# Nine tiles for one ring of raw and compression weights, and an order by due times for DVE, ACT and the load queue

## The chip, the cores and the metric

The kernel runs on one core of a Trainium2 chip. The core has a matrix engine (TensorE, PE in the profile), a vector engine (VectorE, DVE), a scalar engine (ScalarE, ACT), a general one (GpSimd, POOL, hardly used here) and a sync engine (SyncE, SP) from which this kernel issues its loads. Each engine takes its instructions from a queue of its own, in the order in which they were written there, and waits on semaphores for the others. The metric is the device time of one execution in microseconds (us); lower is better.

## What is computed

Two layers, each a token mixer and a squared-ReLU MLP, with RMS norms before and after each, on 256 tokens of width 1024 in float32. The reference, cut to what matters here:

```python
h = rms_norm(x, g_pre_mix)
y = h @ w_in                       # 2848 columns: q, six k/v groups, gates, FoX q, k, v, forget logits
# NSA heads: 8 query heads on 2 k/v heads, three branches added by sigmoid gates
kc = gelu((blocks(k_c) + pos_k) @ w1_k + b1_k) @ w2_k + b2_k     # compressed keys, 15 blocks of 32
vc = gelu((blocks(v_c) + pos_v) @ w1_v + b1_v) @ w2_v + b2_v
o_cmp = masked_softmax(q @ kc.T) @ vc
o_sel = masked_softmax(rope(q) @ rope(k_s).T) @ v_s    # blocks chosen by the compressed scores
o_win = masked_softmax(rope(q) @ rope(k_w).T) @ v_w
# FoX heads: 8, causal attention with a cumulated log forget gate
o_fox = masked_softmax(fq @ fk.T + cum[:, None] - cum[None, :]) @ fv
x = x + rms_norm(concat(o, o_fox) @ w_out, g_post_mix)
h = rms_norm(x, g_pre_mlp)
x = x + rms_norm(square(relu(h @ w_up)) @ w_down, g_post_mlp)
```

With 256 tokens there are four blocks for the selection and 16 may be chosen, so every block is chosen. The window of 512 covers all tokens as well.

## The kernel before

**Precision.** A float32 product is made as three products of a faster type: each operand is split into a high part and a rest, and hi·hi, hi·lo and lo·hi are added up in PSUM (`mm3`). Activations are split once. For weights ACT writes `whi`, a rounded copy of the raw tile, and DVE writes `wlo`, raw minus `whi`, for every weight unit.

**Weights.** All weights come as a list of units in the order in which they are used, most of them 128 partitions by 1024 columns (512 KB). The class `Weights` (from line 414) gives them out: `get(i)` records the load of unit i, unless it was recorded already, and its split. The loads go to SP's queue. A raw unit lands in a tile of the ring with the tag "raw", which has four tiles (`RBUFS`); whi and wlo have seven tiles each (`WBUFS`). The weights of the compression (`w1k` and `w1v`, four units each in a layer) are used by PE as they are, without a split, in one stretch of 16 matmuls each. They have a ring of their own, tag "w1", of four tiles. Their loads are tied to a place in the program by `nc.after` (lines 433 to 443), with the leads `RIDE_LEAD` and `FAR_LEAD`; the units of w1k ride with the four units of chunk 2 of the input projection, those of w1v with chunk 3.

**Stages of a layer.** The columns of `w_in` are cut into six chunks, of which each has four units (the very first chunk eight). Chunks 3 and 4 give the FoX queries and keys transposed (`in_chunk_T`), the others come by token (`in_chunk`), and `evac` functions take them out of PSUM. The rotated queries (`q_rot`: a high part by ACT, a rest by DVE) are transposed by PE, and so are the compressed scores (`csT`, in a tile with the tag "pcT", after `compressed_scores`). Then a loop over 24 score steps (16 for NSA, 8 for FoX) interleaves scores, softmax, transposes and products with the values (`scores`, `scale`, `probs_T`, `pv`); the tiles of probabilities form a ring of three. In its gaps `fill` puts matmuls of the input projection that remain. After that come the output projection, the norms and gains (`pre_gain`, `sandwich`) and the MLP, eight groups of 512 columns.

**Order.** Nothing is put on an engine as the program is written. A `Recorder` (from line 169) writes down every operation with its engine, a `key` (by default its place in the program; loads and splits get the key of an earlier place, `LOAD_LEAD` and `SPLIT_LEAD` units ahead), a cost, the operations that it depends on and the buffers that it uses. Buffers of a ring are given out in order of first use in the program. `order()` (lines 245 to 343) then plays the four queues (tensor, vector, scalar, sync) through at build time, with estimated costs: whenever an engine is free, it takes the operation with the lowest key among those that are ready and whose buffers are free; operations marked urgent come first. `emit` (line 345) writes each engine's instructions in that order. This is why nearly every instruction has line 352 in the profile, and why the profile is read by tile names. The choice stands in one line:

```python
if op.ready <= t and (best is None or (best.urgent, -best.key) < (op.urgent, -op.key)) and fits(op):
```

Of the kernel before, what the change touches and what calls it, by code (L numbers as in the profile page):

```python
# [18 lines left out]
F32 = mybir.dt.float32  # L19
# [5 lines left out]
P = 128  # L25
D = 1024
S = 256
# [5 lines left out]
NEG = -1e30  # L33
LASTK = 4
LANE = 0.9
WAIT = 0.7
WARM = 4
RETILE = 145
# [2 lines left out]
FIRSTS = [(k, k + 1) for k in range(8)]  # L41
NFIRST = 768
UPK = 7
TOK, WBUFS, RBUFS = 6, 7, 4
LOAD_LEAD, SPLIT_LEAD, RIDE_LEAD, FAR_LEAD = 12, 1, 6, 20
OPERANDS = ("whi", "wlo", "xT", "act0", "act1", "qT", "kx0", "kx1", "raw", "w1", "gain", "tok", "rl",
            "pr", "prT", "x0", "x1", "fV", "cum", "cs", "pcT", "vbig", "vS", "vW", "kstk", "kstv", "rT")
EPS = 1e-6

# [67 lines left out]
class Buf:  # L117


    def __init__(self, pool, shape, dtype, name, tag, bufs, psum):  # L120
        self.pool, self.shape, self.dtype, self.name, self.tag, self.bufs = pool, shape, dtype, name, tag, bufs
        self.psum, self.real = psum, None
        self.size = int(np.prod(shape[1:]))
        self.writes, self.reads, self.ops = [], [], 0
# [38 lines left out]

class Op:
    __slots__ = ("engine", "name", "args", "kw", "key", "urgent", "cost", "deps", "succs", "bufs",
                 "missing", "ready", "start", "end", "tile")


class Recorder:
# [21 lines left out]
    def add(self, engine, name, args, kw):  # L191
# [7 lines left out]
        if self.lane is not None and self.key is None:  # L199
            op.key = self.lane + LANE * (len(self.ops) - self.lane)  # L200
        op.urgent = self.hot
# [40 lines left out]
            d.succs.append(op)  # L242
        self.ops.append(op)

    def order(self):


        free = {tag: q[0].bufs for tag, q in self.fifo.items()}
# [25 lines left out]
        def fits(op):  # L274
            taken = {}
            for b in op.bufs:
                if b not in live:
                    n = taken.get(b.tag, 0)
                    if free[b.tag] <= n or self.fifo[b.tag][head[b.tag] + n] is not b:
                        return False  # L280
                    taken[b.tag] = n + 1
            return True
# [3 lines left out]
        count, out, live = 0, [], set()  # L286
        while events:
            t, _, released = heapq.heappop(events)
            if released is not None:
                free[released] += 1  # L290
            if events and events[0][0] == t:
                continue
            for e, ops in waiting.items():
                while busy[e] <= t:
                    best = None
                    for op in ops:
                        if op.ready <= t and (best is None or (best.urgent, -best.key) < (op.urgent, -op.key)) and fits(op):
                            best = op
                    if best is None:
                        break  # L300
                    if not best.urgent and e != "tensor" and not force:
                        q = hot[e]
                        while q and q[0].start is not None:
                            q.popleft()
                        memo = {}
                        if any(estimate(op, memo) < t + WAIT * best.cost for op in list(q)[:4] if op.start is None and fits(op)):
                            break
                    ops.remove(best)
                    for b in best.bufs:
                        if b not in live:  # L310
                            live.add(b)
                            free[b.tag] -= 1
                            head[b.tag] += 1
                    best.start = t
                    out.append(best)
                    if e == "sync":
                        busy[e] = t + 450
                        bus = max(bus, t + 1150) + best.cost
                        best.end = bus + 900
                    else:  # L320
                        busy[e] = best.end = t + best.cost
                        if e == "tensor" and best.tile != tiled:
                            tiled = best.tile
                            busy[e] = best.end = best.end + RETILE
                    count += 1
                    heapq.heappush(events, (busy[e], count, None))
                    for b in best.bufs:
                        left[b] -= 1
                        if not left[b]:
                            count += 1  # L330
                            heapq.heappush(events, (best.end + (260 if b.psum else 150), count, b.tag))
                    for s in best.succs:
                        s.ready = max(s.ready, t, best.end + s.deps[best])
                        s.missing -= 1
                        if not s.missing:
                            waiting[s.engine].append(s)
                            count += 1
                            heapq.heappush(events, (s.ready, count, None))
            force = not events and len(out) < len(self.ops)
            if force:  # L340
                heapq.heappush(events, (t + 100, 0, None))
# [72 lines left out]
class Weights:  # L414


    def __init__(self, nc, tile, units, one, far):
        self.nc, self.tile, self.units = nc, tile, units
        self.raw, self.marks = {}, []

        self.one, self.far = one, far

    def load(self, i):
        kind, shape, src = self.units[i]
        self.raw[i] = (self.tile([P] + shape, F32, name="w1", tag="w1", bufs=4) if kind == "raw" else
                       self.tile([P] + shape, F32, name="wraw", tag="raw", bufs=RBUFS))
        self.nc.sync.dma_start(self.raw[i], src)

    def get(self, i):
        nc, marks = self.nc, self.marks  # L430
        assert len(marks) == i
        marks.append(len(nc.ops))
        if i not in self.raw:
            nc.key = marks[max(i - LOAD_LEAD, 0)]
            far = i in self.far
            if self.units[i][0] == "raw":


                lead = FAR_LEAD if far else RIDE_LEAD
                nc.after = nc.ops[marks[i - lead] - 1] if i > self.one else self.last  # L440
                nc.key = marks[i - lead] if far else nc.key
            self.load(i)
            self.last, nc.after = nc.ops[-1], None
        kind, shape, src = self.units[i]
        raw = self.raw.pop(i)
        nc.key = None
        if kind == "raw":
            return raw
        nc.key = marks[max(i - SPLIT_LEAD, 0)]
        hi = self.tile([P] + shape, F32R, name="whi", tag="whi", bufs=WBUFS)  # L450
        lo = self.tile([P] + shape, F32R, name="wlo", tag="wlo", bufs=WBUFS)
        for j in range(shape[0]) if i < len(FIRSTS) else [slice(None)]:
            if i:
                nc.scalar.activation(hi[:, j], raw[:, j], AF.Copy)
            else:

                nc.vector.tensor_copy(hi[:, j], raw[:, j])
            nc.vector.tensor_sub(lo[:, j], raw[:, j], hi[:, j].bitcast(F32))
        nc.key = None
        return hi, lo  # L460
# [14 lines left out]
def trunk(nc, A, consts_in, out, sbp, pp):  # L475
    def tile(shape, dtype, name, tag=None, bufs=1):
        return nc.tile(sbp[(tag or name) not in OPERANDS], shape, dtype, name, tag, bufs)

# [3 lines left out]
    def small(shape, name, bufs=2):  # L482
        return tile(shape, F32, name=name, tag=name, bufs=bufs)


    units, index = [], {}
# [14 lines left out]
    for l in range(DEPTH):  # L501
        at = 0
        for c, (a, b) in enumerate(CHUNKS):
            w_in = A["w_in"][l][:, at:at + 8 * (b - a)].rearrange("p (k n) -> p k n", k=8)
            at += 8 * (b - a)
            for q, (k0, k1) in enumerate(parts_of(l, c)):
                add_unit((l, "in", c, q), [k1 - k0, b - a], w_in[:, k0:k1, :])
                if (c, q) in RIDES:
                    s, j = RIDES[c, q]
                    w1 = A["cmp_w1_" + s][l].rearrange("p (k n) -> p k n", k=16)  # L510
# [18 lines left out]
            for q in range(4):  # L529
                add_unit((l, "dn", fc, q), [1, D], wd[:, 4 * fc + q:4 * fc + q + 1, :])  # L530

    W = Weights(nc, tile, units, index[0, "out", 0], [index[1, "w1k", j] for j in range(4)])

    def weight(*key):
        return W.get(index[key])
# [13 lines left out]
    for k in range(8):  # L549
# [8 lines left out]
        a = 8 + k * NFIRST - o  # L558
# [172 lines left out]
    xT = new_xT()  # L731
# [14 lines left out]
    for l in range(DEPTH):  # L746
        first = l == 0
# [9 lines left out]
        T = {}  # L757
# [174 lines left out]
        def compressed_scores():  # L932
            ps = psum("s")
            with nc.stretch():
              for p in range(4):
                nc.tensor.matmul(ps[32 * p:32 * p + 32, :S], kbd[:, p // 2].rearrange("p j n -> p (j n)"),
                                 T["qT"][:, p, :], start=True, stop=True, tile_position=(0, 32 * p))
            T["csT"] = small([P, S], "pcT", 1)
            nc.scalar.activation(T["csT"], ps[:, :S], AF.Copy)

        def compressed_exp():
# [343 lines left out]
        for i in range(len(flat) + 4):  # L1285
# [14 lines left out]
            j = i - 3  # L1300
            if 0 <= j < len(flat) and flat[j][2] == 1 and flat[j][3] != 1:
                kind, pair, par, br = flat[j]
# [18 lines left out]
        xT = new_xT()  # L1321
# [106 lines left out]
        for fc in range(8):  # L1428
# [21 lines left out]
            if not last_l:  # L1450
                xT = new_xT()
# [63 lines left out]
```

## Time and profile before

| what | value |
|---|---|
| three runs, median (lowest to highest) | 628.62 us (628.45 to 632.04) |
| the profiled execution | 630.89 us |
| its span in the profile | 629.1 us |
| mean granted clock of TensorE | 0.999 |
| HBM read over the span | 114.00 MB |

The profile shows one execution. Its span leaves out 1.8 us of the time at both ends. A matmul of PE is pipelined with the next and its end is modelled, so the sum of shown durations is more than the distance from one start to the next; distances between starts are the better measure. In rows with tile names, `a<-b,c` is an operation that writes a from b and c; `x2` counts instructions put together in one row. In brackets stands the idle time of the engine just before the row and the operation or transfer that ended it.

### The profile page before, as it was taken

Reading aid. Unit: us, or ns where it says so; the run is one execution under the profiler, and the core shown is the slowest. Engines: PE = TensorE matmul, PEld = TensorE weight load, DVE = VectorE, ACT = ScalarE, POOL = GpSimd, SP = SyncE. Lnnn points to the kernel's source line nnn. Section 1 sums busy time; section 2 is a strip of 40 time slices with the busy share of each in tenths; the row PEclk is TensorE's granted clock in tenths of the full one; section 3 lists DMA queues with packets and bytes.
Section 4 is the critical chain, followed back from the end, with each engine's and each line's share of the span. In section 5 each row is a group of like instructions: output and inputs, shape, how many; then the busy total and the mean of one; then the engine's idle time right before and its main releaser. Section 6 shows DMA issues by size and latency. Waiting matters only on the chain.

```text
span 629.1 us, 9912 instructions
## 1 busy us (share of the span) xinstructions
PE 617.4 (98%) x3572; PEld 518.3 (82%) x3572; DVE 482.4 (77%) x1077; ACT 375.8 (60%) x736; POOL 0.2 (0%) x4
## 2 busy tenths in 40 slices
PE   9999999999999999999999999999999999999995
PEld 7877977788888888888888888777888888888884
DVE  6878999969986566566598999996998666566544
ACT  7855757664865455456468656764767565455432
POOL 0000000000000000000000000000000000000000
PEclk9999999999999999999999999999999999999999
DMA  8986344305777556658326943533268656566501
GB/s 319 379 310 218 100 145 148 130 34 203 236 250 250 195 178 203 193 178 290 122 75 222 329 163 106 158 108 101 68 218 282 220 188 205 187 182 202 190 1 67
DMA packets 33600, 115.69 MB, mean 184 GB/s; under 512 B 3984, under 2 KB 4112, under 8 KB 33552
## 3 DMA queue, kind: packets, MB, share of 16 engines
q1 hardware_dynamic: 33552, 115.07, 55.6%
q8 instruction: 28, 0.46, 0.3%
q14 instruction: 20, 0.16, 0.1%
HBM read 114.00 MB, written 1.05 MB: 183 GB/s over the span
## 4 chain that ended last, share of the span: by engine, by line
PE 81%; DVE 7%; DMA 6%; ACT 4%; issue 1%; DVEq 0%; SPq 0%; ACTq 0%
PE s L352 34%; PE acc L352 24%; PE x L352 18%; DMA wraw<-in_w_in_dram 5%; PE o L352 5%; DVE wlo L352 3%; ACT whi L352 2%; DMA first<-in_first_dram 1%; DVE pr L352 1%; DVE x L352 1%; DVE m L352 1%; ACT xT L352 1%; DVE mg L352 0%; ACT rl L352 0%; DVE rsqrt L352 0%
## 5 line engine op out<-in xcount | busy, mean ns | idle before, releaser
L352 DVE TENSOR_TENSOR wlo<-wraw,whi 128x1024 fp32r<-128x1024 f32 (+1 forms) x188 | 225.0, 1202 | 85.1 <-ACT whi L352 81.9
L352 ACT ACTIVATE whi<-wraw 128x1024 fp32r<-128x1024 f32 (+1 forms) x188 | 194.8, 1041 | 129.3 <-PE acc L352 59.8
L352 PE MATMUL s<-xT,whi 128*128 128x512 f32 x448 | 112.0, 392 | 0.0
L352 PEld LDWEIGHTS s<-xT,whi 128*128 128x128 f32 x448 | 81.5, 189 | 15.1
L352 PE MATMUL acc<-whi,aT 128*128 128x512 f32 x256 | 88.7, 390 | 0.0
L352 PE MATMUL x<-whi,aT 128*128 128x512 f32 x256 | 88.5, 390 | 0.0
L352 PEld LDWEIGHTS s<-xT,wlo 128*128 128x128 f32 x448 | 61.1, 191 | 4.4
L352 PE MATMUL s<-xT,wlo 128*128 128x256 f32 x448 | 62.5, 282 | 0.0
L352 PEld LDWEIGHTS acc<-whi,aT 128*128 128x128 f32 x256 | 48.0, 188 | 9.9
L352 PEld LDWEIGHTS x<-whi,aT 128*128 128x128 f32 x256 | 48.1, 188 | 9.6
L352 ACT ACTIVATE pr<-pr,st 128x128 f32<-128x128 f32 (+1 forms) x96 | 42.8, 448 | 18.1 <-DVE st L352 17.7
L352 PE MATMUL acc<-xT,whi 128*128 128x256 f32 x256 | 50.1, 288 | 0.2 <-DVE fqT L352 0.2
L352 PE MATMUL x<-wlo,aT 128*128 128x512 f32 x128 | 50.0, 391 | 0.0
L352 PE MATMUL acc<-wlo,aT 128*128 128x512 f32 x128 | 49.9, 390 | 0.0
L352 PEld LDWEIGHTS acc<-xT,whi 128*128 128x128 f32 x256 | 40.6, 190 | 2.9 <-issue 1.2
L352 PE MATMUL x<-whi,xT 128*128 128x512 f32 x112 | 37.0, 403 | 0.2 <-ACT xT L352 0.2
L352 PE MATMUL acc<-xT,wlo 128*128 128x256 f32 x128 | 36.3, 284 | 0.0
L352 PE MATMUL acc<-whi,xT 128*128 128x512 f32 (+1 forms) x128 | 35.7, 353 | 0.1
L352 ACT ACTIVATE rl<-x 128x512 f32<-128x512 f32 x24 | 14.7, 614 | 24.9 <-PE x L352 16.7
L352 PEld LDWEIGHTS acc<-wlo,aT 128*128 128x128 f32 x128 | 24.0, 188 | 4.9
L352 PEld LDWEIGHTS x<-wlo,aT 128*128 128x128 f32 x128 | 24.1, 188 | 4.5
L352 ACT ACTIVATE rl<-h 128x512 f32<-128x512 f32 x28 | 17.5, 623 | 16.4 <-DVE h L352 16.4
(230 smaller groups left out, 975.5 us busy)
## 6 DMA issues: line engine op xcount, KB each, us to landing
wraw<-in_w_up_dram SPq DMA_DIRECT2D x64, 512.0 KB, 3.7
wraw<-in_w_down_dram SPq DMA_DIRECT2D x64, 512.0 KB, 3.7
wraw<-in_w_in_dram SPq DMA_DIRECT2D x36, 512.0 KB, 4.5
wraw<-in_w_out_dram SPq DMA_DIRECT2D x16, 512.0 KB, 3.7
w<-in_cmp_w_k_dram SPq DMA_DIRECT2D x8, 512.0 KB, 5.2
w<-in_cmp_w_v_dram SPq DMA_DIRECT2D x8, 512.0 KB, 7.9
first<-in_first_dram SPq DMA_DIRECT2D x7, 384.0 KB, 5.9
wraw<-in_w_in_dram SPq DMA_DIRECT2D x8, 288.0 KB, 4.7
```

Of the source, the lines that this page charges most:

```text
L352: getattr(getattr(self.nc, op.engine), name)(*[real(v) for v in args], **{k: real(v) for k, v in kw.items()})
```

## The change

The change touches the build-time planner and the rings of the loaded weights. What is computed and the operations that are recorded stay the same.

1. The rings "raw" (four tiles) and "w1" (four) become one ring "raw" of nine tiles. The compression weights take their turn in it with the others. The rule that tied their loads to a place (`nc.after`, `one`, `far`, `RIDE_LEAD`, `FAR_LEAD`) is gone; their loads have the same lead as all others.
2. The old `order()` is now `schedule()`, and it takes the lowest `rank` in place of the lowest `key`. The new `order()` plays the queues through once with rank = key. Then `deadlines()` takes TensorE's operations of that result, one after the other without idle time, as due times, and goes backwards through all operations: each is due when the first of its successors is due, less the latency and its own cost; an operation that uses a buffer is also due before the first operation of the buffer that takes over its place in the ring. A load counts 2500 ns more than its transfer (`LANDING`). Operations of DVE, ACT and the load queue get their due time as rank, those of TensorE keep the key. Then the queues are played through once more (`PASSES` = 1).
3. The tile of `csT` gets the tag "cs" in place of "pcT".

```diff
-TOK, WBUFS, RBUFS = 6, 7, 4
-LOAD_LEAD, SPLIT_LEAD, RIDE_LEAD, FAR_LEAD = 12, 1, 6, 20
+PASSES = 1
+LANDING = 2500.0
+TOK, WBUFS, RBUFS = 6, 7, 9
+LOAD_LEAD, SPLIT_LEAD = 12, 1
...
+    def deadlines(self, out):
+        due, t = {}, 0.0
+        for op in out:
+            if op.engine == "tensor":
+                due[op], t = t, t + op.cost
+        taker = {}
+        for q in self.fifo.values():
+            for a, b in zip(q, q[q[0].bufs:]):
+                taker[a] = b
+        first = {}
+        for op in out:
+            for b in op.bufs:
+                first.setdefault(b, op)
+        for op in reversed(out):
+            d = due.get(op, t)
+            cost = op.cost + LANDING if op.engine == "sync" else op.cost
+            for x in op.succs:
+                if x.deps[op] > -1e8 and x in due:
+                    d = min(d, due[x] - x.deps[op] - cost)
+            for b in op.bufs:
+                if taker.get(b) in first and first[taker[b]] in due:
+                    d = min(d, due[first[taker[b]]] - (260 if b.psum else 150) - cost)
+            due[op] = d
+        for op in out:
+            op.rank = op.key if op.engine == "tensor" else due[op]
+
     def order(self):
+        for op in self.ops:
+            op.rank = op.key
+        out = self.schedule()
+        for _ in range(PASSES):
+            self.deadlines(out)
+            out = self.schedule()
+        return out
+
+    def schedule(self):
...
-                        if op.ready <= t and (best is None or (best.urgent, -best.key) < (op.urgent, -op.key)) and fits(op):
+                        if op.ready <= t and (best is None or (best.urgent, -best.rank) < (op.urgent, -op.rank)) and fits(op):
...
     def load(self, i):
         kind, shape, src = self.units[i]
-        self.raw[i] = (self.tile([P] + shape, F32, name="w1", tag="w1", bufs=4) if kind == "raw" else
-                       self.tile([P] + shape, F32, name="wraw", tag="raw", bufs=RBUFS))
+        self.raw[i] = self.tile([P] + shape, F32, name="w1" if kind == "raw" else "wraw", tag="raw", bufs=RBUFS)
...
             nc.key = marks[max(i - LOAD_LEAD, 0)]
-            far = i in self.far
-            if self.units[i][0] == "raw":
-                lead = FAR_LEAD if far else RIDE_LEAD
-                nc.after = nc.ops[marks[i - lead] - 1] if i > self.one else self.last
-                nc.key = marks[i - lead] if far else nc.key
             self.load(i)
-            self.last, nc.after = nc.ops[-1], None
...
-            T["csT"] = small([P, S], "pcT", 1)
+            T["csT"] = small([P, S], "cs", 1)
```

More of the change, by code (lines that the diff above doesn't have):

```diff
@@ L43 @@
 UPK = 7
-TOK, WBUFS, RBUFS = 6, 7, 4
-LOAD_LEAD, SPLIT_LEAD, RIDE_LEAD, FAR_LEAD = 12, 1, 6, 20
-OPERANDS = ("whi", "wlo", "xT", "act0", "act1", "qT", "kx0", "kx1", "raw", "w1", "gain", "tok", "rl",
+TOK, WBUFS, RBUFS = 6, 7, 9
+LOAD_LEAD, SPLIT_LEAD = 12, 1
+OPERANDS = ("whi", "wlo", "xT", "act0", "act1", "qT", "kx0", "kx1", "raw", "gain", "tok", "rl",
             "pr", "prT", "x0", "x1", "fV", "cum", "cs", "pcT", "vbig", "vS", "vW", "kstk", "kstv", "rT")
@@ L165 @@
     __slots__ = ("engine", "name", "args", "kw", "key", "urgent", "cost", "deps", "succs", "bufs",
-                 "missing", "ready", "start", "end", "tile")
+                 "missing", "ready", "start", "end", "tile", "rank")
 class Recorder:
@@ L414, with __init__ @@
 class Weights:
-    def __init__(self, nc, tile, units, one, far):
+    def __init__(self, nc, tile, units):
         self.nc, self.tile, self.units = nc, tile, units
         self.raw, self.marks = {}, []
-        self.one, self.far = one, far
     def load(self, i):
         kind, shape, src = self.units[i]
-        self.raw[i] = (self.tile([P] + shape, F32, name="w1", tag="w1", bufs=4) if kind == "raw" else
-                       self.tile([P] + shape, F32, name="wraw", tag="raw", bufs=RBUFS))
+        self.raw[i] = self.tile([P] + shape, F32, name="w1" if kind == "raw" else "wraw", tag="raw", bufs=RBUFS)
         self.nc.sync.dma_start(self.raw[i], src)
@@ L530, in trunk @@
                 add_unit((l, "dn", fc, q), [1, D], wd[:, 4 * fc + q:4 * fc + q + 1, :])
-    W = Weights(nc, tile, units, index[0, "out", 0], [index[1, "w1k", j] for j in range(4)])
+    W = Weights(nc, tile, units)
     def weight(*key):
```

## The prediction

> **What bounds the kernel now.** I read the page first, then a table of stretches, then the list of what TensorE waited for, then the timelines around each of those waits. The page:
>
> ```profile
> span 629.1 us, 9912 instructions
> ...
> PE 617.4 (98%) x3572; PEld 518.3 (82%) x3572; DVE 482.4 (77%) x1077; ACT 375.8 (60%) x736; POOL 0.2 (0%) x4
> ...
> PE 81%; DVE 7%; DMA 6%; ACT 4%; issue 1%; DVEq 0%; SPq 0%; ACTq 0%
> ```
>
> TensorE is busy 617.4 of 629.1 us. The change alters no computation and adds or removes no instruction that computes, so it can only win from the 11.7 us in which PE is idle, or lose by adding to them. The windows view says where they lie (length, then busy us of PE, PEld, DVE, ACT, POOL, then clock, DMA share, GB/s):
>
> ```profile
> 0.00:40.00 40.00, 38.82 (x217) 31.78 (x218) 31.54 (x95) 30.86 (x64) 0.20 (x4) 1.00 0.93 332
> 40.00:70.00 30.00, 27.08 (x246) 25.07 (x245) 24.32 (x67) 17.58 (x37) 0.00 (x0) 1.00 0.59 202
> 60.00:130.00 70.00, 68.42 (x468) 54.74 (x468) 63.09 (x223) 46.00 (x131) 0.00 (x0) 1.00 0.41 133
> 70.00:130.00 60.00, 59.88 (x397) 46.41 (x396) 54.83 (x192) 38.51 (x113) 0.00 (x0) 1.00 0.46 145
> 130.00:300.00 170.00, 170.00 (x867) 144.97 (x866) 123.79 (x175) 99.58 (x150) 0.00 (x0) 1.00 0.62 203
> 300.00:330.00 30.00, 29.83 (x146) 24.56 (x145) 23.31 (x51) 15.94 (x37) 0.00 (x0) 1.00 0.29 91
> 350.00:380.00 30.00, 29.35 (x262) 26.94 (x260) 27.35 (x76) 17.65 (x38) 0.00 (x0) 1.00 0.69 235
> 370.00:440.00 70.00, 70.00 (x497) 55.94 (x496) 62.52 (x224) 45.34 (x131) 0.00 (x0) 1.00 0.37 111
> 610.00:629.10 19.10, 12.46 (x55) 9.98 (x54) 7.41 (x18) 3.93 (x12) 0.00 (x0) 0.95 0.15 55
> ```
>
> Idle: 1.18 us before 40, 6.64 in the tail after 610, none in the MLP from 130 to 300. Neither the start (warm-up data) nor the tail (the last norm and store) is touched in substance. What a better order can reach is 2.92 + 0.12 + 0.17 + 0.65 = 3.86 us, under 0.7% of the time. The waits of PE name it (total us, times, longest):
>
> ```profile
> PE s L352 <- DVE q_rot L352: 1.9, 2, 1.5
> PE s L352 <- ACT pcT L352: 1.5, 1, 1.5
> PE o L352 <- DVE warm L352: 1.2, 1, 1.2
> PE acc L352 <- DVE fqT L352: 0.2, 1, 0.2
> PE x L352 <- ACT xT L352: 0.2, 1, 0.2
> ```
>
> **Part 1: stall A, the q_rot transposes of layer 0.** Rows of ACT, DVE and PE timelines (start, duration, in brackets the idle before and its releaser):
>
> ```profile
> 43.75 1.06 ACT L352 ACTIVATE whi<-wraw 128x1024 fp32r<-128x1024 f32 x1 [2.42 <-DMA wraw<-in_w_in_dram]
> 44.72 0.61 ACT L352 ACTIVATE q_rot<-q 128x512 fp32r<-128x512 f32 x1
> ...
> 45.36 0.69 DVE L352 TENSOR_TENSOR q_rot<-q,q_rot 128x512 fp32r<-128x512 f32 x1 [2.47 <-ACT q_rot L352]
> ...
> 38.83 0.40 PE L352 MATMUL acc<-xT,whi 128*128 128x256 f32 x2
> ...
> 39.19 0.40 PE L352 MATMUL acc<-xT,whi 128*128 128x256 f32 x2
> ...
> 44.46 0.28 PE L352 MATMUL acc<-xT,wlo 128*128 128x256 f32 x1
> 46.20 1.18 PE L352 MATMUL s<-identr,q_rot 128*128 128x128 f32 x12 [1.46 <-DVE q_rot L352]
> ```
>
> ACT sat 2.42 us behind a weight that had not landed, and q_rot, which PE wanted next, stood behind it in the same queue; DVE then waited 2.47 us for q_rot and PE 1.46. Three 256-wide matmuls take 39.19 − 38.83 = 0.36 us, 0.12 each, so a matmul's shown 0.28 holds 0.16 of modelled tail: the real loss is 46.20 − 44.46 − 0.12 = 1.62 us. In the new order both q_rot copies stand before the splits of the late weights, and PE has about 30 more matmuls ahead of these transposes, 3.6 us at 0.12. The old cause is gone.
>
> What is late next? The one ring. In the order of loads of the changed kernel, five consecutive issues (weight unit 2 of chunk 3, a w1v unit, unit 3 of chunk 3, a w1v unit, unit 0 of chunk 4) stand at or behind a load whose tile holds a w1k unit until the kstk stretch has read it. Rows for this:
>
> ```profile
> 36.51 1.93 PE L352 MATMUL o<-w,kstk 128*32 128x256 f32 x32
> ...
> 23.82 13.33 SPq L352 DMA_DIRECT2D wraw<-in_w_in_dram  x6
> ...
> wraw<-in_w_out_dram SPq DMA_DIRECT2D x16, 512.0 KB, 3.7
> wraw<-in_w_in_dram SPq DMA_DIRECT2D x36, 512.0 KB, 4.5
> ...
> L352 DVE TENSOR_TENSOR wlo<-wraw,whi 128x1024 fp32r<-128x1024 f32 (+1 forms) x188 | 225.0, 1202 | 85.1 <-ACT whi L352 81.9
> L352 ACT ACTIVATE whi<-wraw 128x1024 fp32r<-128x1024 f32 (+1 forms) x188 | 194.8, 1041 | 129.3 <-PE acc L352 59.8
> ```
>
> The stretch ends at 36.51 + 1.93 = 38.4; three of those five loads are among the six that SP issued from 23.82 on. Now SP is held to 38.4. With 3.7 us from issue to landing (nothing else is in flight then, so I take the uncrowded row, not 4.5) the first lands at 42.1, its split is done at 42.1 + 1.04 + 1.20 = 44.4. PE meanwhile has two weight units, 48 matmuls × 0.12 = 5.8 us, and wants it at 44.2: 0.2 late. The following loads land about 0.52 MB / 332 GB/s = 1.6 us apart (the rate of the first window, the densest) against 2.9 us of PE work a unit, and catch up although two of the five are w1v units that PE needs only later; but the second q_rot copy now waits behind the first split on ACT, which I put at another 0.4. So A falls from 1.62 to 0.6: **−1.0**, bounds −1.62 and 0.
>
> The Trainium skill (DMA: Bandwidth & Descriptors, section "Anatomy of one DMA — SWDGE (gpsimd) path") fits a transfer on another issuing path as some 2.0 us plus the bytes at 436 GB/s; by it, as an estimate, 512 KB would land after 3.2 us, the 0.2 would vanish, and the sum below would come out 0.2 lower; the row of 3.7 is this kernel's own and stands.
>
> **Part 2: stall B, the csT transposes.**
>
> ```profile
> 59.78 1.06 ACT L352 ACTIVATE whi<-wraw 128x1024 fp32r<-128x1024 f32 x1 [2.99 <-DMA wraw<-in_w_in_dram]
> ...
> 61.13 0.36 ACT L352 ACTIVATE pcT<-s 128x256 f32<-128x256 f32 x1
> ...
> 59.80 0.28 PE L352 MATMUL acc<-xT,wlo 128*128 128x256 f32 x1
> 61.54 0.44 PE L352 MATMUL s<-cst,pcT 128*128 128x128 f32 x2 [1.46 <-ACT pcT L352]
> ```
>
> Again ACT is held, 2.99 us, by a unit that PE needs ten us later, and the copy of the compressed scores stands behind. Real loss 61.54 − 59.80 − 0.12 = 1.62. In the new ring that unit takes the tile of unit 0 of chunk 4, where it took that of unit 1: free one unit of PE work sooner, 24 matmuls × 0.12 = 2.9 us, about the length of ACT's idle; and ranked by due time the copy goes before a split that is due later. The new tag of csT ("cs", one tile) costs nothing: the next user of that tile is the DVE addition that reads what these transposes put out, so it waits for them already. I leave 0.2 for a pr exp ahead of it: **−1.4**, bounds −1.62 and −0.8 (a whole split still ahead).
>
> **Part 3: stalls C and D in layer 1.**
>
> ```profile
> 353.85 1.06 ACT L352 ACTIVATE whi<-wraw 128x1024 fp32r<-128x1024 f32 x1 [1.22 <-DMA wraw<-in_w_in_dram]
> ...
> 356.30 0.85 PE L352 MATMUL s<-identr,q_rot 128*128 128x128 f32 x8 [0.41 <-DVE q_rot L352]
> ...
> 365.93 0.50 PE L352 MATMUL acc<-xT,whi 128*128 128x256 f32 x2 [0.24 <-DVE fqT L352]
> ```
>
> C is A again with a shorter hold: 0.41 + 0.16 = **−0.57**, bounds −0.57 and 0. D waits for a PSUM bank; in the new order the kstv stretch (as long as kstk's, 1.93) moves ahead of it, which covers 0.24 + 0.16 = **−0.4**, bounds −0.4 and 0. The wait on xT at the layer boundary stays: its chain (norm, merge, transposes) gets one split more on DVE and one weight unit more on PE ahead of it.
>
> **Part 4: what is moved into the way.** Places change for 894 of 3150 recorded PE operations, 667 of 981 on DVE, 358 of 607 on ACT, 95 of 233 loads, none by more than 36. Three spots have little cover; two of their rows, from the groups of lines in 60 to 130 (busy, mean ns, idle before and its releaser):
>
> ```profile
> L352 ACT ACTIVATE oT<-o 128x512 fp32r<-128x512 f32 x4 | 2.4, 594 | 5.9 <-PE o L352 5.9
> ...
> L352 DVE TENSOR_TENSOR xo<-x,gains 128x1024 f32<-128x1024 f32 x2 | 2.4, 1204 | 0.0
> ```
>
> (a) Near 110, a 1.04 us split is put ahead of an oT copy that PE's output stage waits for: 0 to 1.04, I take 0.4, since ACT stood idle 5.9 us before four such copies, waiting for PE, which covers most of it. (b) In layer 1 near 407 the 1.2 us xo multiplication moves ten places forward on DVE, ahead of score scaling, and itself waits for the gains to land: 0 to 1.2, I take 0.3. (c) At 338 to 340, wlo steps stand ahead of the rope steps of the K heads; one 1.2 us wlo against a cover of half a microsecond that the next PE group gives: 0 to 0.7, I take 0.2. Loads of bias, w2 and constants pass behind five weight loads on SP, but their users are moved later too: nothing. Before layer 1 SP waits for tiles as before and nine units are ahead instead of four plus four of w1: nothing, since PE did not wait for a weight there. Together **+0.9**, bounds 0 and +2.9.
>
> **Sum.** −1.0 − 1.4 − 0.57 − 0.4 + 0.9 = −2.5. The profiled execution took 630.89 us (span 629.1 and 1.8 outside); less 2.5 is 628.4. It lay 2.27 above the median of 628.62, so the forecast for the median is 628.62 − 2.5 = **626.1 us**.
>
> **Rivals.**
>
> (1) The ring gives back what the order wins: no net change, 628.6. SP is in order, and it does wait at its head for a tile:
>
> ```profile
> SPq L352 <- DVE wlo L352: 357.3, 130, 17.6
> ```
>
> If the five held loads land at 5.3 us instead of 3.7 after 38.4, A is back whole (0.2 + 0.4 + 1.6 > 1.62), and with bounds of part 4 at half (+1.5) the total is −1.4 − 0.57 − 0.4 + 0.6 + 1.5 ≈ 0. For it: w_in units took 4.5 on the median. Against: those shared the engines with other loads at a DMA share of 0.93. The same section of the Trainium skill says that DMA engines do not wait on semaphores and that the issuing sequencer does, before dispatch: by that rule everything behind the held load is late too, as reckoned here, and SP's waits in the row agree.
>
> (2) DVE becomes the bound in the score loops: slower. In 60–130 it is busy 63.09 of 70 us, in 370–440 62.52 of 70, slack 6.9 and 7.5. Each loop has 24 score steps on a pr ring of three. The due times bring DVE's score steps up to 29 places forward (at 63.09/223 = 0.28 us a place), while PE's matching transposes go up to 31 places back; a DVE operation at the head of its queue that waits for PE blocks the wlo behind it. At w us lost in each step, 24w beyond the slack becomes PE time; it decides from w = 6.9/24 = 0.29. At w = 0.6, half a wlo, an estimate: 2 × 14.4 − 6.9 − 7.5 = +14.4, so 626.1 + 14.4 = 640.5. Against: steps only move by due time within what PE's own sequence allows, and PE has hardly a wait in either loop today.
>
> (3) All named stalls vanish and nothing new comes: −1.62 − 1.62 − 0.57 − 0.4 = −4.2, 624.4.
>
> **How the numbers follow.** Forecast 0.52, rival (1) 0.24, (3) 0.13, (2) 0.11. Low end: all 3.86 us shown idle, plus 0.16 of tail at six stalls, gone: −4.8, so 623.8, and a quarter of the 2.27 us by which single executions differ: 623.2. High end: rival (1) with part 4 at its upper bound: 628.6 + 2.9 − 0.5 = 631.0. About 0.13 lies outside, nearly all of it above. A change of under 1% can't be told from none here (622.3 to 634.9): faster 0.04, since even the low end doesn't reach 622.3; slower 0.09, rival (2) past its break-even; within 0.87.
>
> **What would show it.** Right: PE's waits on q_rot under 0.8 us and on pcT under 0.3, PE busy unchanged near 617 and idle in 40–70 near 1.2 us; ACT without a 2 to 3 us hold by a landing between 40 and 62; SP waiting until about 38.4 in layer 0. Rival (1) would show a PE wait on a whi or wlo near 44; rival (2) DVE idle in 60–130 put down to PE, and new PE waits on pr or prT. The forecast falls if the clock or the tail moves, or if PE, with the same instructions in another order, is busy more than 1 us longer or shorter.

## The result and the profile after

| | before | after |
|---|---|---|
| times, median (lowest to highest) | 629.13 us (627.72 to 632.04, 10 runs) | 626.05 us (625.65 to 626.77, 10 runs) |
| profiled execution, span | 630.89, 629.1 us | 626.18, 624.4 us |

The ratio after to before is 0.9948, with a 95% interval from 0.9932 to 0.9964: 3.3 us of 629.13, faster by half a per cent. The forecast was 626.1. The medians differ by 3.1 us, the two profiled spans by 4.7. Why these two numbers differ is the first question for the experiments.

The page of the changed kernel (all recorded instructions now have line 392):

```profile
span 624.4 us, 9952 instructions
...
PE 615.1 (99%) x3572; PEld 517.5 (83%) x3572; DVE 481.0 (77%) x1077; ACT 378.4 (61%) x736; POOL 0.2 (0%) x4
...
PE 91%; DVE 4%; DMA 2%; ACT 1%; issue 1%; DVEq 0%; SPq 0%
```

The chain that ended last is on PE for 91% of the span, 81% before; transfers and ACT hold 3% of it, where they held 10%. (A second profile of the kernel before, below, has PE at 96% of its chain, so this share does not tell the two kernels apart.) Idle time of PE is 624.4 − 615.1 = 9.3 us (11.7 before). Beside that PE is busy 2.3 us less with the same 3572 matmuls. The windows say where the idle time went (length, PE, PEld, DVE, ACT, POOL, clock, DMA share, GB/s):

```profile
40.00:70.00 30.00, 30.00 (x271) 28.03 (x271) 26.13 (x74) 20.94 (x41) 0.00 (x0) 1.00 0.71 262
70.00:130.00 60.00, 59.64 (x388) 46.57 (x387) 56.60 (x200) 39.96 (x119) 0.00 (x0) 1.00 0.46 146
...
330.00:350.00 20.00, 19.52 (x135) 15.61 (x135) 16.53 (x53) 12.94 (x26) 0.00 (x0) 1.00 0.71 240
350.00:380.00 30.00, 30.00 (x270) 27.90 (x269) 27.79 (x78) 18.95 (x43) 0.00 (x0) 1.00 0.80 283
```

From 40 to 70 PE has no gap left, where it had 2.92 us; from 350 to 380 none, where it had 0.65. New are 0.36 in the first score loop and 0.48 at 336. PE's list of waits gives them names:

```profile
PE o L392 <- DVE warm L392: 1.2, 1, 1.2
PE s L392 <- DVE kW L392: 0.5, 1, 0.5
PE x L392 <- ACT oT L392: 0.4, 1, 0.4
PE x L392 <- ACT xT L392: 0.3, 1, 0.3
PE x L392 <- DVE oT L392: 0.2, 1, 0.2
```

q_rot, pcT and fqT are gone. The place of stall A, from the timelines of SP, ACT and PE:

```profile
28.24 0.33 SPq L392 DMA_DIRECT2D w<-in_cmp_w_v_dram  x1
34.48 0.33 SPq L392 DMA_DIRECT2D wraw<-in_w_in_dram  x1
...
33.78 1.93 PE L392 MATMUL o<-w,kstk 128*32 128x256 f32 x32
...
41.55 1.06 ACT L392 ACTIVATE whi<-wraw 128x1024 fp32r<-128x1024 f32 x1 [0.53 <-DMA wraw<-in_w_in_dram]
42.93 0.63 ACT L392 ACTIVATE q_rot<-q 128x512 fp32r<-128x512 f32 x1 [0.32 <-DVE q L392]
...
47.75 1.14 PE L392 MATMUL s<-identr,q_rot 128*128 128x128 f32 x12
```

SP does stand from 28.6 to 34.48, for a tile that a w1k unit holds, as the prediction had it for the one ring. But the stretch starts at 33.78, 2.7 us sooner than before, and each tile comes free when its own matmuls are done, not at the end of the stretch. The second q_rot copy is done at 43.6, and PE comes to the transposes at 47.75 without a wait.

### The profile page after: what moved, and what is told of

It is laid out like the page before. It is cut to its first block, busy times and chain, and to the rows that moved or that the text cites. A ratio compares the mean times of both kernels' runs of the same rounds, so it can differ in the third digit from the quotient of the medians.

```text
span 624.4 us, 9952 instructions
## 1 busy us (share of the span) xinstructions
PE 615.1 (99%) x3572; PEld 517.5 (83%) x3572; DVE 481.0 (77%) x1077; ACT 378.4 (61%) x736; POOL 0.2 (0%) x4
## 4 chain that ended last, share of the span: by engine, by line
PE 91%; DVE 4%; DMA 2%; ACT 1%; issue 1%; DVEq 0%; SPq 0%
PE s L392 34%; PE acc L392 28%; PE x L392 24%; PE o L392 6%; DVE pr L392 2%; DMA wraw<-in_w_in_dram 1%; DVE wlo L392 1%; DMA first<-in_first_dram 1%; ACT whi L392 1%; ACT rl L392 0%; DVE cum L392 0%; DVE prT L392 0%; DVE st L392 0%; DVE prX L392 0%; ACT xT L392 0%
## 5 line engine op out<-in xcount | busy, mean ns | idle before, releaser
L392 ACT ACTIVATE pr<-pr,st 128x256 f32<-128x256 f32 (+1 forms) x96 | 42.9, 450 | 15.6 <-DVE st L392 14.3
L392 PE MATMUL acc<-xT,whi 128*128 128x256 f32 x256 | 48.8, 286 | 0.0
```

The source lines that it names most:

```text
L392: getattr(getattr(self.nc, op.engine), name)(*[real(v) for v in args], **{k: real(v) for k, v in kw.items()})
```

## The experiments

Each row was timed side by side with the kernel before, and its ratio is to those times (medians of 629.13 to 630.16 us), so rows are compared by ratio rather than by median.

| kernel | median us | ratio, 95% interval |
|---|---|---|
| the whole change | 626.05 | 0.9948, 0.9932 to 0.9964 |
| before, three splits of ACT moved | 627.45 | 0.9966, 0.9952 to 0.9979 |
| one ring, old keys | 627.82 | 0.9964, 0.9950 to 0.9978 |
| one ring, due times for loads only | 627.81 | 0.9965, 0.9951 to 0.9979 |
| one ring, due times for DVE and ACT only | 628.65 | 0.9982, 0.9972 to 0.9992 |
| old rings, due times | 635.43 | 1.0093, 1.0076 to 1.0110 |
| the same, xo later | 629.94 | 1.0001, 0.9989 to 1.0012 |
| nine tiles in two rings, due times | 630.98 | 1.0025, 1.0008 to 1.0042 |
| one ring of eight | 627.97 | 0.9969, 0.9959 to 0.9980 |
| the change, LANDING 0 | 625.87 | 0.9939, 0.9925 to 0.9952 |
| the change, planned with later landings | 627.55 | 0.9961, 0.9941 to 0.9981 |
| the change, one split moved | 626.36 | 0.9946, 0.9931 to 0.9961 |

**The kernel before, once more.** No edit.

> The kernel before, unchanged, for a second profiled execution of it. Its ten times reach from 627.72 to 632.04 us (4.3 us), those of the changed kernel from 625.65 to 626.77 (1.1 us). Theory: the stalls at q_rot and pcT hang on when a transfer lands, so they differ from execution to execution: PE's waits on q_rot and pcT come to between 1.0 and 3.4 us in all here (3.4 in the first profile), and the span follows them within 0.5 us. Rival: the scatter comes from somewhere else (start, tail, clock): both waits stand within 0.2 us of the first profile though the span differs by over 1 us.

It took 628.03 us, with a span of 626.3. From its timelines of ACT and PE, at the places of stalls A and B:

```profile
42.52 1.06 ACT L352 ACTIVATE whi<-wraw 128x1024 fp32r<-128x1024 f32 x1 [1.05 <-DMA wraw<-in_w_in_dram]
...
44.97 1.19 PE L352 MATMUL s<-identr,q_rot 128*128 128x128 f32 x12
...
56.84 1.06 ACT L352 ACTIVATE whi<-wraw 128x1024 fp32r<-128x1024 f32 x1 [1.28 <-DMA wraw<-in_w_in_dram]
...
58.70 0.38 PE L352 MATMUL s<-cst,pcT 128*128 128x128 f32 x2
```

The same program, but the unit that held ACT until 43.75 in the first profile is there at 42.52. Of A 0.29 us is left, under the modelled end of the matmul ahead (it starts at 44.56), and of B nothing. Of the waits that the list shows on q_rot and pcT only 0.5 us is left (that in layer 1), 2.9 less than in the first profile, below the expected range; the span is 2.8 less, as the theory had it. The chain that ended last is on PE for 96% of this span. So stalls A and B come and go with the landing of a transfer, and the profiled execution from which the prediction was made was one that had both.

**Three instructions moved.**

```diff
+            for a, b in self.late.items():
+                out.remove(self.ops[a])
+                out.insert(out.index(self.ops[b]) + 1, self.ops[a])
...
+    W.holds = {index[0, "in", 4, 1]: ("q_rot", 0), index[1, "in", 4, 3]: ("q_rot", 1), index[0, "in", 5, 2]: ("cs", 0)}
```

Each split named in `holds` (`a` in the loop) goes directly behind the copy named beside it (`b`): unit 1 of chunk 4 behind q_rot in layer 0, unit 3 of chunk 4 behind q_rot in layer 1, unit 2 of chunk 5 behind the copy to csT in layer 0.

> The kernel before with three instructions of ACT moved and nothing else: the split of unit 1 of chunk 4 behind the second q_rot copy in layer 0, that of unit 3 of chunk 4 behind it in layer 1, and that of unit 2 of chunk 5 behind the copy of the compressed scores in layer 0. Theory (the gain is the held queue of ACT, stalls A, B and C): of the 3.8 us that they cost in the first profile most goes, 2.5 to 3.8 us less than before, ratio 0.994 to 0.996, and PE waits neither for q_rot nor for pcT over 0.3 us. Rival (the gain comes from the rings and the new order as a whole): under 1 us, ratio 0.9985 or more, with the waits turned into others nearby.

0.9966, that is 2.1 us, a little under the expected 2.5 to 3.8; its ten times reach from 626.89 to 628.74, 1.9 us where the kernel before had 4.3, so more than half of the scatter went with the stalls. PE waits for neither copy any more. Three places in ACT's queue carry about two thirds of the gain, 2.1 of 3.3 us, though the intervals overlap.

**The ring alone.** `PASSES = 0`.

> The changed kernel without the second pass: one ring of nine, no ties for the compression weights, csT in cs, and the old keys as rank. In its order on ACT both q_rot copies and the copy of the compressed scores already stand ahead of the late splits. Theory (what counts is that order around the three stalls): about all of the gain, 625.5 to 627.0 us, ratio 0.994 to 0.997. Rival (the due times carry the gain): 628 to 629, ratio 0.998 or more.

0.9964: the ratio is in the range of the theory, the median 0.8 us above its times. Most of the gain is there, not all: the slowest time of the whole change, 626.77, lies below the fastest here, 627.38. Without any due time ACT has both q_rot copies ahead of the split that waits for its transfer; the second copy and that split:

```profile
40.56 0.63 ACT L392 ACTIVATE q_rot<-q 128x512 fp32r<-128x512 f32 x1
43.87 1.06 ACT L392 ACTIVATE whi<-wraw 128x1024 fp32r<-128x1024 f32 x1 [2.67 <-DMA wraw<-in_w_in_dram]
```

ACT is held longer here than at stall A of the first profile (2.67 us after 2.42), and PE waits for neither q_rot nor csT: what stands behind the held split decides, not the hold.

**Due times alone.** Rings, ties and leads of before.

> The changed kernel with the rings of before (four raw tiles, four of the compression weights, their loads tied as before), so due times alone, and csT in cs. Its order on ACT has the second q_rot copy behind one split fewer and the compressed scores ahead of the late split. Theory (the order around the stalls): most of the gain, 626.0 to 627.5 us, ratio 0.995 to 0.998. Rival (the ring with loads in order of use carries the gain): 628 to 630, ratio 0.999 or more.

Both theories failed: 1.0093, slower by 5.9 us. The timelines of SP, DVE and PE show one place:

```profile
98.18 0.33 SPq L392 DMA_DIRECT2D gains<-in_g_pre_mlp_dram  x1
...
105.63 1.23 DVE L392 TENSOR_TENSOR xo<-x,gains 128x1024 f32<-128x1024 f32 x1 [3.81 <-DMA gains<-in_g_pre_mlp_dram]
...
107.73 0.92 PE L392 MATMUL s<-cst,pr 128*128 128x128 f32 x3 [4.04 <-DVE pr L392]
```

The due times bring xo forward on DVE, and on the old rings the gains are issued late and land 7.4 us after that. DVE stands at xo, the score steps stand behind it, and PE stands 4.04 us. The windows of the same run show what follows (clock is the third number from the end):

```profile
103.00:107.00 4.00, 0.69 (x3) 0.21 (x2) 1.37 (x4) 1.06 (x1) 0.00 (x0) 0.97 0.72 245
107.00:109.00 2.00, 1.08 (x4) 0.66 (x5) 2.00 (x9) 1.58 (x4) 0.00 (x0) 0.50 0.04 16
109.00:111.00 2.00, 2.00 (x13) 1.67 (x12) 2.00 (x8) 1.60 (x7) 0.00 (x0) 0.50 0.00 0
111.00:113.00 2.00, 2.00 (x13) 1.08 (x11) 1.88 (x10) 0.93 (x6) 0.00 (x0) 0.50 0.43 98
113.00:115.00 2.00, 2.00 (x24) 1.50 (x22) 1.51 (x4) 0.16 (x2) 0.00 (x0) 0.85 0.45 178
```

PE's granted clock falls to 0.50 within the pause and stays there until about 113.6, so the matmuls after it are slower too. PE is busy 620.5 us in this run and 618.1 in the next, which has no such pause: by this difference, an estimate, some 2.4 us on top of the 4.04.

**The same with xo later.**

```diff
             due[op] = d
+            if op.engine == "vector" and op.args and isinstance(op.args[0], View) and op.args[0].buf.name == "xo":
+                due[op] += 8000.0
```

> Due times with the rings of before, as in the run of due times alone (ratio 1.0093), but the product of the residual with the gains (xo) counts 8 us later as due, which puts it about 12 operations of DVE further back in layer 0. There DVE stood 3.81 us at xo for gains that had not landed, PE stood 4.04 us for a pr behind it, and PE's granted clock then was 0.50 for some 6 us. Theory (that one wait and the clock after it make the loss): PE waits for no pr over 0.5 us near 103, the clock stays at 1.00 from 95 to 130, and the ratio falls by 0.009 to 0.014, to 0.995 to 1.000. Rival (due times on four raw tiles lose everywhere): the ratio stays above 1.004.

1.0001: the ratio falls by 0.009, the wait of 4.04 us and the half clock are gone. What is left of due times on the old rings is no gain, with PE waits on h, st, oT and others of 0.2 to 0.7 us in place of A and B.

**Due times for one part only.**

```diff
-            op.rank = op.key if op.engine == "tensor" else due[op]
+            op.rank = due[op] if op.engine in ("vector", "scalar") else op.key     # or: == "sync"
```

> The changed kernel with due times for DVE and ACT alone; the loads keep their old keys. The ring alone gave 0.9964, the whole change 0.9948, about 1 us more. Theory (the rest comes from what DVE and ACT do first): 0.994 to 0.9955 here, and PE's excess over its steady pace in the first 130 us is like that of the changed kernel. Rival (it comes from the order of the loads): 0.996 or more.

> The changed kernel with due times for the loads alone; DVE and ACT keep their old keys. Theory (the rest comes from what DVE and ACT do first): 0.996 to 0.9975, as with the ring alone. Rival (it comes from the order of the loads): 0.9955 or less.

0.9982 and 0.9965: neither brings more than the ring alone, and the first brings less, though its interval just touches that of the ring alone. Neither the order on DVE and ACT nor that of the loads holds the rest by itself. Of these orders only the one that ranks loads, DVE and ACT together has it.

**Nine tiles in two rings.** w1 units get a tag of their own again, with four tiles; raw has five.

> The changed kernel with its nine tiles in two rings again, five for raw weights and four for the compression weights, without the old ties: due times and storage as in the change, but not one ring in order of use. Theory (what is won hangs on copies standing ahead of splits on ACT, and here they do for q_rot in layer 0 and for the compressed scores): 0.994 to 0.997. Rival (the order that the one ring forces on the loads is needed beside due times, as the slow run with the old rings suggests): 0.999 or more, with a wait of DVE or ACT on a landing that PE feels.

1.0025, the number of the rival. Neither arrangement of two rings, with the old ties or without, gains anything from due times, so of those tried the one ring is needed. But the place is not a wait on a landing, as the rival had it, from the timelines of ACT and PE:

```profile
27.56 0.60 ACT L392 ACTIVATE kx<-s 128x512 fp32r<-128x512 f32 x1 [2.72 <-PE s L392]
...
29.73 3.90 ACT L392 ACTIVATE whi<-wraw 128x1024 fp32r<-128x1024 f32 x4
...
30.83 0.73 PE L392 MATMUL x<-whi,xT 128*128 128x512 f32 x2 [1.01 <-ACT whi L392]
```

Here it is the copy that stands in the way: ACT waits 2.72 us at kx for PE, four splits stand behind it, and then PE waits 1.01 us for the first of them. That is the longest new wait of PE, and not the whole loss.

**One ring of eight**, and **LANDING 0**: one constant each.

> The changed kernel with eight tiles in the one ring, the storage of before. Theory (one tile fewer issues each load one unit later, about 1.3 to 2.9 us, and the order is planned anew around it): 0.995 to 0.998, no single wait of PE over 0.8 us. Rival (the ninth tile is what keeps transfers ahead of the splits): 0.999 or more.

> The changed kernel with 0 in place of 2500 ns for LANDING, so a load counts as due 2.5 us later. On ACT the order around the three stalls is the same. Theory (the ring sets the order of most loads, which is the order of use already): within 0.001 of the change, 0.994 to 0.9958. Rival (loads that are due earlier are what the due times bring): 0.9965 or more.

0.9969 and 0.9939, both as the theory had it, the second but for 0.0001. With eight tiles, the storage of before, three fifths of the gain are there. LANDING makes no difference that these intervals can tell; 625.87 is the lowest median of all, but its interval covers that of the change.

**Two tries to win more.** The kW wait at 336 looked like the old fault at a new place: rows of ACT and PE of the changed kernel:

```profile
334.08 1.06 ACT L392 ACTIVATE whi<-wraw 128x1024 fp32r<-128x1024 f32 x1 [1.45 <-DMA wraw<-in_w_in_dram]
335.05 0.35 ACT L392 ACTIVATE kstk<-s 64x240 f32<-64x240 f32 x1
...
336.11 0.30 PE L392 MATMUL s<-cst,kW 128*128 128x128 f32 x1 [0.48 <-DVE kW L392]
```

The first try puts that one split behind the copies to kstk, kW and kx; the second plans all transfers 1 us longer (`best.end = bus + 1900` in place of `bus + 900`).

> The changed kernel with one instruction of ACT moved: in layer 1, near 334, the split that waited 1.45 us for its transfer goes behind the copies to kstk, kW and kx that stood behind it. Theory (the new wait of PE on kW, 0.48 us shown, is the old fault at a new place: a split that waits for a landing ahead of copies that PE needs): that wait is gone, 0.3 to 0.7 us less than the changed kernel, ratio 0.9935 to 0.9945. Rival (the split steps of DVE ahead of the rope steps make it, as the prediction had it): the wait stays within 0.2 us.

The kW wait is gone, so the cause was right, but the time is not better, 0.9946. PE's list has a new entry in its place:

```profile
PE s L396 <- DVE q_rot L396: 0.4, 1, 0.4
```

> The changed kernel, planned with transfers that land 1 us later. A median unit took 3.7 us from issue to landing, up to 6.2 in groups; splits should then be placed where their weight is there, and fewer of them hold ACT. Theory (waits for a landing ahead of copies are what is left to win): PE's waits on kW and oT, 0.84 us shown, fall by half, 0.993 to 0.9945. Rival (a new order trades these waits for others, as in the run with one split moved): 0.9945 to 0.9965.

0.9961, the rival: the kW wait is gone here too, PE waits on oT at two places and on prX instead. Neither beats the change.

## Why the prediction was right, and where it was not

**Stall A.** Sized at −1.0 with a residue of 0.6 from the ring; in the profiled execution of the change all 1.62 us of the first profile are gone. The step that failed is that SP is held to 38.4, the end of the stretch at its old place. It is held to 34.48. The landing and the spacing were right: the first of the five loads landed 3.6 us after its issue (3.7 predicted), and ACT, waiting for both, starts the splits of unit 3 of chunk 3 and unit 0 of chunk 4 at 41.55 and 44.11, and with a w1v load between them that is 1.3 us a load (1.6 predicted).

**Stalls B, C and D.** −1.4, −0.57 and −0.4 predicted; no bracket is left at any of them. (The tile in part 2 is that of unit 1 of chunk 4 in place of unit 2: the prediction numbered both one too low.)

**New waits.** +0.9 predicted. Shown are 0.36 and 0.2 at oT, 0.48 at kW and 0.1 more on xT, 1.1 together. For (a), at oT, 0.4 was taken, but no split stands there: ACT was idle 1.06 us for PE, and PE had two matmuls fewer between the product and its use. For (b), where 0.3 was taken, there is no wait in the change; that its risk is real is what the run of due times alone shows, in layer 0. For (c) the size was 0.2, and the cause was named wrongly: not wlo steps on DVE, but a split on ACT that waited for its transfer.

**The sum.** That 626.05 met 626.1 is luck in part: the median of before came out 0.5 us higher than the 628.62 of the prediction, and the gain between medians 0.6 larger than the 2.5 forecast. −2.5 was taken off a median, though its terms came from one execution. A and B were worth 3.24 us there, and 0.3 in the second profile. At the median the three moved splits are worth 2.1 us where the prediction had 1.0 + 1.4 + 0.57 = 2.97. The total came out near because another term was missing: 3.3 − 2.1 − 0.4 (D) + 1.1 (new waits) = 1.9 us are none of the named stalls, by the middle of intervals that are each about 1 us wide to either side. The prediction named busy time of PE that changes by over 1 us as a sign against it, and it did: 615.1 after 617.4, while the ring alone has 617.1. Part of it are waits too short to show, since a matmul's modelled end covers them. PE's rows at the start of chunk 1, first the ring alone, then the change:

```profile
16.79 0.51 PE L392 MATMUL acc<-whi,xT 128*128 128x288 f32 x2
17.39 0.40 PE L392 MATMUL acc<-wlo,xT 128*128 128x288 f32 x1
```

```profile
16.36 0.42 PE L392 MATMUL acc<-whi,xT 128*128 128x288 f32 x2
16.62 0.29 PE L392 MATMUL acc<-wlo,xT 128*128 128x288 f32 x1
```

Two matmuls take 0.60 us in the one and 0.26 in the other; 0.34 us, with no bracket. About 0.25 of it is a wait for wlo, whose step on DVE ends at 17.33; the rest follows the two rsqrt matmuls that stand just ahead here, and that the change has further back.

Where the change gains on the ring alone can be read from a point at which both have done the same work. When the first MLP begins, the same 888 matmuls are behind every order; the next one, first in the change, then in the ring alone:

```profile
132.38 0.62 PE L392 MATMUL s<-whi,xT 128*128 128x512 f32 x2
```

```profile
133.80 0.73 PE L392 MATMUL s<-whi,xT 128*128 128x512 f32 x2
```

The change is 1.42 us ahead there and 1.3 at its last matmul, so the lead is made in the mixer of layer 0: 0.75 after 65 matmuls (17.41 and 18.16), and 0.6 more in the score loop after 72. The runs with LANDING 0 and with one split moved, whose order is nearly that of the change, are at 132.60 and 132.47; due times for loads alone at 133.91, for DVE and ACT alone at 134.57. So this part is in three executions and no accident of one, and layer 1 adds nothing to it on balance. Which wait or order of matmuls makes it, and why it needs due times on all queues together, was not shown and stays open.

**The range.** The high end of 631.0 does not follow from its terms. Rival (1) with part 4 at +2.9 is −1.4 − 0.57 − 0.4 + 0.6 + 2.9 = +1.1, which gives 629.8. The result lies far from it.

**The rivals.** The ring does not give back what the order wins; it is what makes the order safe. The slower rival, DVE waiting for PE at many of 24 score steps, does not show in the change: PE has one wait of 0.36 us in that loop of layer 0. On the old rings DVE did block the score loop, by another mechanism: one wait of 3.81 us on a transfer, with the clock after it. The third, all stalls gone and nothing new, was right on the stalls and wrong by the 1.1 us of new waits.

## What to carry to other kernels

An instruction that waits for a transfer holds everything behind it on its engine; look at what stands behind each such wait, and who needs it, before buying bandwidth or buffers. A stall that hangs on a landing is not in every execution: take a second profile before its size is taken off a median, and count the scatter that it makes, 4.3 us here against 1.1 without it, as a sign of it. Ranking work by when it is needed can put a step ahead of the landing of its input, and here one such step (xo) made nearly all of a loss of 0.9%. Due times paid only with the one ring, and only when the loads and their users were ranked together.

## What the runs showed of the hardware

PE's granted clock stayed at 1.00 through pauses of 1.62 us in the kernel before. In one of 4.04 us, from 103.7 to 107.7, it fell to 0.50, from about 106.7 to 113.6 (0.97 over 103 to 107 and 0.85 over 113 to 115 in the windows above), and then came back. The Trainium skill ("TensorE: Matmul & The Clock Gate", section "What's actually happening") has the clock halved after at least one idle window of some 3.4 us and full again after at least one busy window as long. The runs agree: the pause of 1.62 us left the clock alone and that of 4.04 did not, and PE had worked some 5.9 us, with gaps, when the clock came back.
